# Hybrid decoder trunk: the norm scales of four norms spread through DRAM, the first SSD transposes tied behind products

## The chip, the cores and the metric

The kernel runs on one core of one Trainium2 chip. The metric is the device time of one execution in microseconds (us), taken as the median of several runs. The kernel before takes 2185.96, 2186.17 and 2187.34 us, median 2186.17. The profiled execution, which all rows of the profile come from, took 2185.88 us; its span from the first to the last instruction is 2184.1 us, with a mean granted TensorE clock of 0.999.

Engines are named as in the profile: PE is TensorE (PEld its weight loads), DVE is VectorE, ACT is ScalarE, POOL is GpSimd, SP is SyncE. An L with a number is a line of the kernel.

## The reference

The trunk has two residual layers for 256 tokens of width 2048, all in float32. Each layer is a mixer and a gated FFN, each behind an RMS norm; a last norm closes it.

```python
def rms_norm(x, w):
    xf = x.astype(jnp.float32)
    y = xf * lax.rsqrt(jnp.mean(xf * xf, axis=-1, keepdims=True) + EPS)
    return (y * w.astype(jnp.float32)).astype(x.dtype)
...
    for layer in range(DEPTH):
        hn = rms_norm(h, mix_norm_w[layer])
...
        h = h + mix.astype(h.dtype)
        f = conv_ffn(rms_norm(h, ffn_norm_w[layer]), ffn_w_gate[layer], ffn_w_up[layer],
                     ffn_conv_w[layer], ffn_conv_b[layer], ffn_w_down[layer])
        h = h + f.astype(h.dtype)
    return rms_norm(h, final_norm_w)
```

The even layer's mixer is stick-breaking attention beside a Mamba-2 SSD, the odd layer's a mixture of dilated attentions. The even mixer projects the input to q, k, v, a gate z, the SSD's inputs (through a causal convolution of width 4 and a SiLU) and 16 step sizes dt. The SSD part has a norm of its own (`ssm_norm_w`).

## The kernel before

Activations lie transposed: 16 tiles of 128 channels by 256 tokens. Every weight panel comes from DRAM in chunks of 128 x 1024 values (512 KB). `prep` (L135) loads one chunk by SP into one of 4 `raw` buffers, ACT casts it to a high half (L153), DVE subtracts to get the low half (L154), both into one of 3 `hl` buffers. `chan` (L218) then multiplies: 16 products per chunk, two accumulator banks, for each weight tile one product of the high half with both halves of x (512 columns) and one of the low half with the high half of x (256 columns), L225. 78% of the chain of work that ended last is L225.

The norm is not applied to x before the products. The weight of the norm goes into x; the factor per token (1 over the root of the mean square) is multiplied onto the results. `square` sums the squares; `stats` (L313) makes the scale: a product with a column of 1/D sums over the partitions (L321), then thirteen small DVE steps (L323, and L305 to L311 in `rsqrt`) give `rcol`, the scale with tokens on partitions, 128 x 2 values. The results have channels on partitions and need the scale along the free dimension, the same on all partitions: `rbc`, 128 x 256. `stats` makes it by two PE products of a broadcast column of `rcol` with the identity (L329, each two records in the trace) and an ACT copy out of PSUM (L333). `token_scale` (L336) runs `stats` in the background of the products, with `gap` ticks (one per chunk) between the two parts. It is used by the even mixer, both FFNs and the odd mixer. The SSD's inner norm calls `stats` itself (L1067). That makes five norms; the final norm is computed another way.

Uses of `rbc`: in the even mixer L904 and L922 (convolution inputs and gates, both DVE), in the FFN L671 (DVE) and L678 (POOL), in the odd mixer L839 and L845 (DVE).

The even mixer begins with `opening` (L165), 16 steps that compute the first values, dt, and four tiles of the convolution's inputs at once; its `token_scale` starts late, since the squares are summed during the opening. Right behind it stand, on DVE and ACT, the reading of the first values (L885, L887), the sums of the accumulators (L288 on ACT, L289 on DVE), the convolution (L904, ACT L907, three L909 per tile, ACT L911), the decays of the SSD (L948 to L968, then three products L974, L975, L977 and a trip of the row sums through DRAM, written by ACT at L984 and read back to all partitions by four POOL transfers of 512 KB at L989), and the casts and low halves of the next chunks.

`ssd` (L991) first transposes eight tiles, each in two halves of the tokens, in four groups of four (L1003, one PSUM bank per group), and DVE multiplies each group by dt (L1008).

The order on each engine is not the order of the source: a scheduler lays the instructions out, by priorities and its own estimates of time, wherever their inputs allow. `issue_after(i)` forbids it to place an instruction ahead of instruction `i`. So the first group of transposes, whose inputs are ready early, stands far ahead of the code around it. Engines run their list in order; semaphores make them wait for each other and for transfers.

Of the kernel before, what the change touches and what calls it, by code (L numbers as in the profile page):

```python
# [9 lines left out]
F32 = mybir.dt.float32  # L10
# [5 lines left out]
P = 128  # L16
T = 256
NT = T // P
# [50 lines left out]
class Trunk:  # L69
# [148 lines left out]
    def chan(self, accs, hl, xs, k0, start, stop):  # L218


        for nt in range(2):
            for k in range(CH):
                for w in range(2):
                    n = (2 - w) * T
                    self.nc.tensor.matmul(  # L225
                        accs[nt][:, :n], hl[w][:, k, nt * P : (nt + 1) * P], xs[k0 + k][:, :n],
                        start=start and k == w == 0, stop=stop and w == 1 and k == CH - 1,
                    )
# [81 lines left out]
            v.tensor_tensor(t, t, x, ALU.mult)  # L310
            v.scalar_tensor_tensor(y, t, 1.5, y, ALU.add, ALU.mult)  # L311

    def stats(self, sums, inv):  # L313


        nc = self.nc
        s = sums[0]
        self.then(nc.vector, "tensor_tensor", s[:, :T], s[:, :T], s[:, T:], ALU.add)
        ps = self.psum()
        for tt in range(NT):  # L320
            nc.tensor.matmul(ps[:, tt : tt + 1], s[:, tt * P : (tt + 1) * P], inv[:, 0:1], start=True, stop=True)  # L321
        ms = self.norm_tile("ms", NT)
        nc.vector.tensor_scalar(ms, ps[:, :NT], EPS, None, ALU.add)  # L323
        col = self.norm_tile("rcol", NT)
        self.rsqrt(col, ms, NT)
        yield col
        pb = self.psum()
        for tt in range(NT):
            nc.tensor.matmul(  # L329
                pb[:, tt * P : (tt + 1) * P], col[:, tt : tt + 1].broadcast_to([P, P]), self.ident, start=True, stop=True  # L330
            )
        bc = self.norm_tile("rbc")
        nc.scalar.copy(bc, pb[:, :T])  # L333
        yield bc

# [655 lines left out]
    def ssd(self, dt, o):  # L991


        nc = self.nc
        v = nc.vector
        conv = self.conv

        xdt = []
        for tt in range(NT):
            for g in range(2):  # L1000
                ps = self.psum()
                for i in range(4):
                    nc.tensor.transpose(  # L1003
                        ps[:, i * P : (i + 1) * P], conv[4 * g + i][:, tt * P : (tt + 1) * P], self.ident
                    )
                t = self.big("ssd", 14, F32)
                h0 = tt * SSH + 8 * g
                v.tensor_tensor(  # L1008
                    t.rearrange("p (h c) -> p h c", c=SSP), ps.rearrange("p (h c) -> p h c", c=SSP),
                    dt[:, h0 : h0 + 8].unsqueeze(2).broadcast_to([P, 8, SSP]), ALU.mult,  # L1010
                )
                xdt.append(t)
                yield
# [3 lines left out]
        for g in range(2):  # L1017
            b, cc = conv[8 + g], conv[10 + g]
            ps = self.psum()
            nc.tensor.matmul(ps[:, :T], b[:, :P], cc, start=True, stop=True)  # L1020
            nc.tensor.matmul(ps[:, T:W], b[:, P:], cc[:, P:], start=True, stop=True)
            t = self.t256("sc", 2, W)
# [6 lines left out]
        sums = []  # L1029
        ys = []  # L1030
        for j in range(SSH // 2):
            g = j // 4
# [4 lines left out]
            for i in range(2):  # L1037
                h = 2 * j + i
                for c in range(NT):
                    col = self.sums[:, c * SSH + h : c * SSH + h + 1]  # L1040
# [23 lines left out]
                self.square(sums, self.convs[j // 2])  # L1064
        yield
        yield
        st = self.stats(sums, self.invi)  # L1067
        next(st)
        yield
        yield  # L1070
        rbc = next(st)
        for j in range(8):
            t = self.t256("cv", 3)
# [173 lines left out]
```

## Time and profile before

| what | us |
|---|---|
| runs: lowest, median, highest | 2185.96, 2186.17, 2187.34 |
| profiled execution | 2185.88 |
| its span | 2184.1 |
| PE busy | 2174.2 |
| DVE busy | 1517.5 |
| ACT busy | 1167.1 |
| POOL busy | 96.8 |
| L225 products of x and panels: one record, mean | 0.333 |
| L329: 20 records, busy in all | 3.0 |
| L1003: 16 records, busy in all | 2.7 |

Matmuls are pipelined, so the duration of one record is longer than the distance between two starts; the chain of waits, which counts each stretch of time once, is better for prices. A line of the timeline holds the start, the duration, the engine, the line, the operation with its output and inputs, and in brackets the idle time before it with what ended it. A line of the chain holds start, time on the chain, engine, what is written and the line.

### The profile page before, as it was taken

To read this page: it belongs to the slowest core of one execution; us is meant where nothing else is said; L and a number is where in the kernel's file an instruction comes from. 1 tells how busy PE (TensorE), PEld (TensorE's weight loads), DVE (VectorE), ACT (ScalarE), POOL (GpSimd) and SP (SyncE) were. 2 spreads that over 40 slices of the span, in tenths; PEclk is the share of its full clock that TensorE was granted. 3 is DMA by queue.
4 is the path that set the end of the run, shared out by engine and by line. 5 is a ranking of instruction groups with operands and counts; after the bars stand their busy time and mean duration, and the time that the engine had idled before them with its cause. 6 is when DMAs were issued, how large, how long until landed. Compare 5 with 4: busy or idle time off the path is not lost.

```text
span 2184.1 us, 33866 instructions
## 1 busy us (share of the span) xinstructions
PE 2174.2 (100%) x13129; PEld 1934.0 (89%) x13129; DVE 1517.5 (69%) x2294; ACT 1167.1 (53%) x1709; POOL 96.8 (4%) x107
## 2 busy tenths in 40 slices
PE   9999999999999999999999999999999999999998
PEld 8888888888888888888888888888888888888998
DVE  8688766776767665555565556667676766687887
ACT  7566554655555554444454454546555555555554
POOL 0000000110101010000000000000010101000000
PEclk9999999999999999999999999999999999999999
DMA  7755566666666666666656555666666666666665
GB/s 252 242 173 151 168 187 192 191 193 194 194 195 193 195 194 194 193 193 194 193 175 181 175 172 177 184 193 189 185 193 193 194 193 194 194 202 199 206 205 162
DMA packets 117713, 417.54 MB, mean 191 GB/s; under 512 B 13072, under 2 KB 15408, under 8 KB 117552
## 3 DMA queue, kind: packets, MB, share of 16 engines
q1 hardware_dynamic: 116352, 412.48, 62.4%
q8 instruction: 102, 1.67, 0.3%
q0 software_dynamic: 576, 2.10, 0.3%
q10 hardware_dynamic: 624, 0.81, 0.1%
q14 instruction: 59, 0.48, 0.1%
HBM read 413.22 MB, written 2.11 MB: 190 GB/s over the span
## 4 chain that ended last, share of the span: by engine, by line
PE 98%; DVE 1%; ACT 0%; DMA 0%; issue 0%; SPq 0%; DVEq 0%
PE acc L225 78%; PE acc L518 5%; PE acc L424 4%; PE acc L526 3%; PE aux L542 2%; PE acc L542 1%; PE acc L235 1%; PE acc L198 1%; PE acc L242 1%; PE acc L190 0%; PE aux L779 0%; PE aux L810 0%; PE acc L200 0%; PE aux L801 0%; PE aux L1057 0%; DMA raw<-in_wfirst 0%
## 5 line engine op out<-in xcount | busy, mean ns | idle before, releaser
L225 PE MATMUL acc<-x,hl 128*128 128x512 f32 (+1 forms) x7680 | 1319.5, 333 | 0.3 <-DVE hl L154 0.3
L154 DVE TENSOR_TENSOR hl<-raw,hl 128x1024 fp32r<-128x1024 f32 x740 | 905.8, 1224 | 580.2 <-ACT hl L153 573.1
L225 PEld LDWEIGHTS acc<-x,hl 128*128 128x128 f32 x7680 | 1156.3, 188 | 151.1 <-issue 0.7
L153 ACT CAST hl<-raw 128x1024 fp32r<-128x1024 f32 x740 | 776.7, 1050 | 766.4 <-PE acc L225 530.4
L225 PE MATMUL acc<-act,hl 128*128 128x512 f32 (+1 forms) x1408 | 239.5, 332 | 0.0
L225 PEld LDWEIGHTS acc<-act,hl 128*128 128x128 f32 x1408 | 212.0, 188 | 27.4
L225 PE MATMUL acc<-o,hl 128*128 128x512 f32 (+1 forms) x1024 | 175.1, 333 | 0.0
L225 PEld LDWEIGHTS acc<-o,hl 128*128 128x128 f32 x1024 | 154.2, 188 | 20.0
L288 ACT COPY ev<-acc 128x256 f32<-128x256 f32 x244 | 90.8, 374 | 149.5 <-PE acc L225 148.5
L678 POOL TENSOR_TENSOR cv<-cv,rbc 128x256 f32<-128x256 f32 x88 | 93.6, 1082 | 1228.9 <-ACT cv L677 1228.9
L518 PE MATMUL acc<-hl,act 128*128 128x256 f32 x998 | 119.8, 278 | 0.0
L518 PEld LDWEIGHTS acc<-hl,act 128*128 128x128 f32 x998 | 117.4, 188 | 0.4
L289 DVE TENSOR_TENSOR ev<-acc,ev 128x256 f32<-128x256 f32 x244 | 102.2, 420 | 5.2 <-ACT ev L288 3.3
L424 PE MATMUL acc<-hl,x 128*128 128x512 f32 x384 | 90.5, 393 | 0.0
L424 PEld LDWEIGHTS acc<-hl,x 128*128 128x128 f32 x384 | 71.5, 188 | 14.8
L526 PE MATMUL acc<-hl,act 128*128 128x512 f32 x264 | 60.0, 389 | 0.0
L526 PEld LDWEIGHTS acc<-hl,act 128*128 128x128 f32 x264 | 49.5, 188 | 10.3
L688 DVE TENSOR_TENSOR ev<-ev,cv 128x256 f32<-128x256 f32 x88 | 38.3, 437 | 12.0 <-DVE ev L289 2.3
L677 ACT ACTIVATE cv<-cv,params 128x256 f32<-128x256 f32 x88 | 40.1, 503 | 0.1
L674 ACT ACTIVATE cv<-pad,params 128x256 f32<-128x256 f32 x88 | 39.9, 505 | 0.0
L671 DVE TENSOR_TENSOR pad<-ev,rbc 128x256 f32<-128x256 f32 x88 | 37.5, 426 | 3.0
L675 DVE SCALAR_TENSOR_TENSOR cv<-pad,params,cv 128x256 f32<-128x256 f32 x88 | 38.5, 479 | 0.0
(224 smaller groups left out, 1210.0 us busy)
## 6 DMA issues: line engine op xcount, KB each, us to landing
raw<-in_wg SPq DMA_DIRECT2D x176, 512.0 KB, 4.2
raw<-in_wu SPq DMA_DIRECT2D x176, 512.0 KB, 4.1
raw<-in_wd SPq DMA_DIRECT2D x176, 512.0 KB, 4.3
raw<-in_wev SPq DMA_DIRECT2D x76, 512.0 KB, 4.1
raw<-in_wod SPq DMA_DIRECT2D x64, 512.0 KB, 3.7
raw<-in_wevo SPq DMA_DIRECT2D x32, 512.0 KB, 4.2
raw<-in_wodv SPq DMA_DIRECT2D x32, 512.0 KB, 3.6
raw<-in_wodo SPq DMA_DIRECT2D x32, 512.0 KB, 3.6
```

The lines of the kernel that those rows point to most:

```text
L153: nc.scalar.copy(hi, raw)
L154: self.lo = nc.vector.tensor_tensor(lo, raw, hi.bitcast(F32), ALU.subtract)
L225: self.nc.tensor.matmul(accs[nt][:, :n], hl[w][:, k, nt * P : (nt + 1) * P], xs[k0 + k][:, :n], start=start and k == w == 0, stop=stop and ...
L288: nc.scalar.copy(t, acc[:, T:])
L289: nc.vector.tensor_tensor(t, acc[:, :T], t, ALU.add)
L424: self.nc.tensor.matmul(acc, part(xs[k0 + k], p), hl[:, k, w, :], start=start and n == k == 0, stop=stop and n == 2 and k == ch - 1,)
L518: mm(block(accs, tt, j), x, both(hl, w, k)[:, j], start=first, stop=stop and k == 1 and i == 2 and (two or j == 1),)
L526: mm(accs[tt][0].rearrange("p (j c) -> p j c", c=T), part(xs[2 * pair + k], p, tt), both(hl, w, k), start=start and i == k == 0, stop=stop ...
L542: mm(m[i] if i in m else block(accs, *own[i]), x[p], w[b][q], start=start and n == 0 and i not in own, stop=stop and n == 2 and i not in own)
L674: nc.scalar.activation(c, gp[:, 2:], AF.Copy, scale=w(2))
L677: self.last = nc.scalar.activation(c, c, AF.Silu, bias=self.par("fcb", l * FT + j))
L678: nc.gpsimd.tensor_tensor(c, c, self.rbc, ALU.mult)
```

## The change

Four norms (all with `token_scale`) no longer spread their scale by PE. Right after `rcol`, `stats` issues two transfers from POOL: one writes the 256 values to a DRAM tile, the other reads them back as one row for all 128 partitions, into `rbc`. The products L329 and the copy L333 remain only for the SSD's norm, which passes `soon=True`. The transposes of `ssd` are tied behind the last panel product that had been written when their code ran (`self.mm`).

```diff
@@ chan
-                    self.nc.tensor.matmul(
+                    self.mm = self.nc.tensor.matmul(
@@ stats
-    def stats(self, sums, inv):
+    def stats(self, sums, inv, soon=False):
...
         self.rsqrt(col, ms, NT)
+        bc = self.norm_tile("rbc")
+        if not soon:
+            back = self.dram.tile([NT, P], F32, name=self.nm("cols"))
+            nc.gpsimd.dma_start(back.rearrange("t p -> p t"), col)
+            nc.gpsimd.dma_start(bc, back.rearrange("t p -> (t p)").unsqueeze(0).broadcast_to([P, T]))
         yield col
+        if not soon:
+            yield bc
         pb = self.psum()
...
-        bc = self.norm_tile("rbc")
         nc.scalar.copy(bc, pb[:, :T])
@@ ssd
-                    nc.tensor.transpose(
-                        ps[:, i * P : (i + 1) * P], conv[4 * g + i][:, tt * P : (tt + 1) * P], self.ident
-                    )
+                    with self.tc.issue_after(self.mm.ins):
+                        nc.tensor.transpose(
+                            ps[:, i * P : (i + 1) * P], conv[4 * g + i][:, tt * P : (tt + 1) * P], self.ident
+                        )
@@ ssd, its norm
-        st = self.stats(sums, self.invi)
+        st = self.stats(sums, self.invi, soon=True)
```

Lines of the changed file are higher by 7 or 8 behind `stats`: L904 is L911 there, L909 is L916, L922 is L929, L951 and L952 are L958 and L959, L968 is L975, L974 is L981, L1003 is L1011; the two transfers are L330 and L331.

The change moves instructions. First DVE, just after the opening, before the change; `hl_666` is the weight buffer of chunk 2 of the products behind the opening (the count starts at 0), `rbc_548` the spread scale:

```order
L289 TENSOR_TENSOR ev_645<-acc_141,ev_645 128x256
L289 TENSOR_TENSOR ev_655<-acc_142,ev_655 128x256
L904 TENSOR_TENSOR pad_135<-ev_645,rbc_548 128x256
L904 TENSOR_TENSOR pad_136<-ev_655,rbc_548 128x256
L951 TENSOR_SCALAR s_601<-s_598 128x32
L154 TENSOR_TENSOR hl_666<-raw_665,hl_666 128x1024
L952 RECIPROCAL s_601<-s_601 128x32
```

And the same place after the change, where chunk 2's buffer is called `hl_665` and the scale `rbc_507`:

```order
L289 TENSOR_TENSOR ev_644<-acc_141,ev_644 128x256
L289 TENSOR_TENSOR ev_654<-acc_142,ev_654 128x256
L154 TENSOR_TENSOR hl_665<-raw_664,hl_665 128x1024
L958 TENSOR_SCALAR s_600<-s_597 128x32
L911 TENSOR_TENSOR pad_135<-ev_644,rbc_507 128x256
L959 RECIPROCAL s_600<-s_600 128x32
L911 TENSOR_TENSOR pad_136<-ev_654,rbc_507 128x256
```

The low half of chunk 2 now stands ahead of the two products with the scale. Some thirty rows further on DVE, before the change, with chunk 4's buffer `hl_742` and chunk 5's `hl_763`:

```order
L968 SCALAR_TENSOR_TENSOR s_620<-dt_134,s_618 128x16 x2
L909 SCALAR_TENSOR_TENSOR cv_691<-pad_135,params,cv_691 128x256
L909 SCALAR_TENSOR_TENSOR cv_701<-pad_136,params,cv_701 128x256
L289 TENSOR_TENSOR ev_729<-acc_575,ev_729 128x256
L909 SCALAR_TENSOR_TENSOR cv_701<-pad_136,params,cv_701 128x256
L922 TENSOR_TENSOR ev_729<-ev_729,rbc_548 128x256
L909 SCALAR_TENSOR_TENSOR cv_701<-pad_136,params,cv_701 128x256
L289 TENSOR_TENSOR ev_734<-acc_576,ev_734 128x256
L154 TENSOR_TENSOR hl_742<-raw_741,hl_742 128x1024
L922 TENSOR_TENSOR ev_734<-ev_734,rbc_548 128x256
L154 TENSOR_TENSOR hl_763<-raw_762,hl_763 128x1024
```

The same rows of DVE after the change, where these buffers are `hl_741` and `hl_762`:

```order
L975 SCALAR_TENSOR_TENSOR s_619<-dt_134,s_617 128x16 x2
L916 SCALAR_TENSOR_TENSOR cv_690<-pad_135,params,cv_690 128x256
L154 TENSOR_TENSOR hl_741<-raw_740,hl_741 128x1024
L916 SCALAR_TENSOR_TENSOR cv_690<-pad_135,params,cv_690 128x256
L916 SCALAR_TENSOR_TENSOR cv_700<-pad_136,params,cv_700 128x256
L289 TENSOR_TENSOR ev_728<-acc_574,ev_728 128x256
L916 SCALAR_TENSOR_TENSOR cv_700<-pad_136,params,cv_700 128x256
L929 TENSOR_TENSOR ev_728<-ev_728,rbc_507 128x256
L916 SCALAR_TENSOR_TENSOR cv_700<-pad_136,params,cv_700 128x256
L289 TENSOR_TENSOR ev_733<-acc_575,ev_733 128x256
L154 TENSOR_TENSOR hl_762<-raw_761,hl_762 128x1024
L929 TENSOR_TENSOR ev_733<-ev_733,rbc_507 128x256
```

Chunk 4's low half has moved up by seven operations of the convolution and the gates; chunk 5's has kept its place. Now PE, where chunk 4 begins, before the change (`acc_739` and `acc_740` are the two banks of the second job):

```order
L225 MATMUL acc_739<-x_151,hl_742 128x512
L225 MATMUL acc_740<-x_151,hl_742 128x512
L974 MATMUL aux_911<-s_620,consts 128x32
L975 MATMUL aux_911<-s_620,consts 128x16
L977 MATMUL aux_914<-consts,s_620 32x128
L1003 MATMUL aux_1378<-consts,ssd_644 128x128 x2
L1003 MATMUL aux_1378<-consts,ssd_686 128x128 x2
L225 MATMUL acc_739<-x_151,hl_742 128x256
```

After the change the three products of the decays stand one chunk later on PE (chunk 5, `hl_762`):

```order
L225 MATMUL acc_739<-x_207,hl_741 128x256
L225 MATMUL acc_738<-x_233,hl_762 128x512
L225 MATMUL acc_739<-x_233,hl_762 128x512
L981 MATMUL aux_910<-s_619,consts 128x32
L982 MATMUL aux_910<-s_619,consts 128x16
L984 MATMUL aux_913<-consts,s_619 32x128
L225 MATMUL acc_738<-x_233,hl_762 128x256
```

The first group of transposes has left that place. It now stands 382 panel products further on PE, at the end of a chunk and one chunk ahead of the second group:

```order
L225 MATMUL acc_1271<-x_465,hl_1336 128x512
L225 MATMUL acc_1271<-x_465,hl_1336 128x256
L1011 MATMUL aux_1377<-consts,ssd_643 128x128 x2
L1011 MATMUL aux_1377<-consts,ssd_685 128x128 x2
L225 MATMUL acc_1384<-x_151,hl_1387 128x512
L225 MATMUL acc_1384<-x_151,hl_1387 128x256
```

The other three groups stand where they stood. On ACT the four copies L333 are gone and some of the casts and copies near the opening change places; on POOL the two transfers of each norm stand ahead of that norm's first use.

## The prediction

> **What bounds the kernel now.** I read the page first: its span, its busy time by engine and the chain of work that ended last; then the groups of instructions for the product that the change removes.
>
> ```profile
> span 2184.1 us, 33866 instructions
> ...
> PE 2174.2 (100%) x13129; PEld 1934.0 (89%) x13129; DVE 1517.5 (69%) x2294; ACT 1167.1 (53%) x1709; POOL 96.8 (4%) x107
> ...
> PE 98%; DVE 1%; ACT 0%; DMA 0%; issue 0%; SPq 0%; DVEq 0%
> ...
> L329 PE MATMUL aux<-consts,rcol 128*128 128x128 f32 x20 | 3.0, 273 | 0.0
> ```
>
> TensorE (PE) carries 98% of the chain, so time is won only where PE has less to do or waits less. The removed product is 20 records, four for each of five norms. The change takes four norms' worth. Next, the chain of waits around such a product at the start of the first FFN:
>
> ```profile
> 373.91 4.08 PE acc L225 x24
> 377.99 0.44 PE aux L329 x4
> 378.44 13.62 PE acc L225 x80
> ```
>
> Here PE runs without a gap: a panel product takes 4.08/24 = 0.170 us, a chunk of 16 takes 2.72, and one norm's spreading product takes 0.44. Then the one stretch in which PE is not the bound, the start of the even mixer, in the same view:
>
> ```profile
> 37.69 0.47 ACT hl L153
> ...
> 38.64 0.36 ACT rbc L333
> 39.01 0.74 ACT v L885 x2
> 39.75 0.61 ACT ev L288 x3
> ...
> 40.69 0.94 ACT hl L153
> ...
> 41.88 0.33 DVE hl L154
> ...
> 43.01 0.35 DVE s L952
> ...
> 47.63 1.14 DVE hl L154
> ...
> 52.96 1.14 DVE hl L154
> ...
> 54.15 3.91 PE acc L225 x22
> ```
>
> From 37.69 to 54.15 the chain runs through ACT and VectorE (DVE). DVE has the convolution, the decays and the low halves of the weights (L154) to do in one order, and PE waits for the low half of chunk 4, which is written only at 52.96. I count chunks of the products from 40.20 on, from 0. The timeline of PE shows that wait:
>
> ```profile
> 51.73 0.30 PE L974 MATMUL aux<-s,consts 128*128 128x32 f32 x2
> 51.87 0.37 PE L975 MATMUL aux<-s,consts 128*128 128x16 f32 x2
> 52.17 0.41 PE L977 MATMUL aux<-consts,s 128*32 128x128 f32 x2
> 52.51 0.55 PE L1003 MATMUL aux<-consts,ssd 128*128 128x128 f32 x3
> 53.56 0.33 PE L1003 MATMUL aux<-consts,ssd 128*128 128x128 f32 x1 [0.50 <-ACT ssd L911]
> 54.15 0.38 PE L225 MATMUL acc<-x,hl 128*128 128x256 f32 x1 [0.26 <-DVE hl L154]
> ```
>
> The four early transposes (L1003) show a wait of 0.50 us for ACT, which is what the tie seems to remove. But behind them stands the later wait, for DVE: without the transposes PE would still resume at 54.15.
>
> **The products removed.** In the FFNs and the odd mixer they lie on the chain: 3 x 0.44 = 1.32 us gained, as long as the scales arrive in time. In the opening the fourth gains nothing at first. The timeline there, of DVE and of PE's weight loads:
>
> ```profile
> 39.91 0.37 DVE L887 SCALAR_TENSOR_TENSOR dt<-acc,rcol,params 128x16 f32<-128x16 f32 x2
> ...
> 40.20 4.79 PEld L225 LDWEIGHTS acc<-x,hl 128*128 128x128 f32 x28 [0.27 <-DVE dt L887]
> ```
>
> PE already waits at 40.20 for DVE's reading of the first values (L887). DVE is held by an L154 that follows the cast of 37.69, and that cast waits for a product that stands before L329. Ending the opening 0.44 earlier lengthens this wait. The copies L333 are hidden behind PE, except in the opening, where 0.36 us leave the ACT chain.
>
> **The order on DVE.** The order of the changed program (shown with the change) puts the third L154 ahead of the two products with the scale, and the L154 of chunk 4 ahead of seven operations of the convolution. The three products of the decays move behind chunk 4. So take one state: all of chunk 4, two products of chunk 5 and the three decay products are done. Before: 54.15 + 16 x 0.170 = 56.87. After: 82 products from 40.20, at the 0.175 us that the 66 before 51.73 took (11.53/66), plus 52.51 - 51.73 = 0.78, is 55.3. DVE must also have the low half of chunk 5 ready; before, it follows that of chunk 4:
>
> ```profile
> 54.33 2.37 DVE L154 TENSOR_TENSOR hl<-raw,hl 128x1024 fp32r<-128x1024 f32 x2
> ```
>
> The first of these two is chunk 5's, done at about 55.5. Its place in the list of DVE is nearly the same in both orders, so it comes at 55.5 again if DVE has not stood still meanwhile. The stretch gains 56.87 - 55.5 = 1.4 us, less the time d that DVE loses by waiting for the scale.
>
> **The tie.** The four moved transposes now stand where PE never waits. The chain gives their price from the second group:
>
> ```profile
> 121.98 0.44 PE aux L1003 x4
> ```
>
> So +0.44 us, certain. DVE reads their result only behind the second group's, whose place is unchanged, so nobody waits longer for them.
>
> **The trip through DRAM.** This decides d, and no row shows it: a POOL transfer of 256 values of 4 bytes, POOL's wait for it, and a POOL transfer of 128 KB. When must it be back? The last step of the scale on DVE and its first use, in the opening and in the first FFN:
>
> ```profile
> 36.31 0.16 DVE L311 SCALAR_TENSOR_TENSOR rcol<-nt,rcol 128x2 f32<-128x2 f32 x1
> ...
> 40.86 0.75 DVE L904 TENSOR_TENSOR pad<-ev,rbc 128x256 f32<-128x256 f32 x2
> ...
> 375.64 0.16 DVE L311 SCALAR_TENSOR_TENSOR rcol<-nt,rcol 128x2 f32<-128x2 f32 x1
> ...
> 383.89 0.43 DVE L671 TENSOR_TENSOR pad<-ev,rbc 128x256 f32<-128x256 f32 x1
> ```
>
> In the first FFN there are 8.1 us (383.89 - 375.80), and PE keeps a finished chunk in hand behind that; the odd mixer and the second FFN have the same pattern. On POOL the second transfer waits for the first; behind it stand only work of 55.38 (opening) and the FFN's products with the scale, which come after that use, so this wait delays nobody else. In the opening the scale is ready at 36.47. In the new order the use follows the third L154: the ACT pair L885 ends at 39.4 without L333, two of the L288 at 39.8, the cast at about 40.85, L154 and a small step at 42.2 or 42.3. So 5.8 us are free there, and each us beyond holds DVE, with every L154 queued behind it. The nearest rows for the price, from timeline, transfers and line views:
>
> ```profile
> 53.68 0.34 ACTq L984 DMA_DIRECT2D rows<-s  x1
> ...
> DMA to landing us min/median/max: 1.4/1.4/1.4
> ...
> 55.38 2.29 POOL L989 DMA_DIRECT2D sr<-rows  x4 [54.30 <-DMA rows<-s]
> ...
> L989 POOL DMA_DIRECT2D sr<-rows x4: 527/532/720, 55.4 to 57.1; - x4
> ...
> raw<-in_wev SPq DMA_DIRECT2D x7, 512.0 KB, 4.2
> ...
> sr<-rows POOLq DMA_DIRECT2D x4, 512.0 KB, 11.2
> ```
>
> A 16 KB write from ACT lands 1.4 us after its issue, and POOL follows 0.3 later. As quick a trip is 2 x (0.3 + 1.4) = 3.4 us. With a weight load's 4.2 for each it is 2 x (0.3 + 4.2) = 9.0. The 11.2 belongs to four broadcasts of 512 KB that crowd each other; I leave it as a far end. I take 2.8 per transfer, the middle of 1.4 and 4.2, since these are small but run beside the weights and are issued by POOL: 2 x (0.3 + 2.8) = 6.2 us. The scale is back at 36.47 + 6.2 = 42.7, so d = 0.4; at 3.4 us d = 0, at 9.0 us d = 3.2.
>
> The Trainium skill, "DMA: Bandwidth & Descriptors", section "Anatomy of one DMA — SWDGE (gpsimd) path", gives about 2.0 us fixed plus the bytes at 436 GB/s for a POOL transfer; by it the trip is an estimated 4.9 us with my waits, d is 0 and the sum 0.4 us better. No run here shows a POOL transfer of this size.
>
> **Sum.** -1.32 (three products) + 0.44 (transposes) - 1.4 + 0.4 (the stretch) = -1.9 us. The profiled execution took 2185.88 us, 1.78 more than its span; that makes 2184.0. The median of the runs is 0.29 higher, so 2184.3.
>
> **Rivals.** (1) *The trip is long and DVE becomes the wait.* For it: five L154 queue behind the waiting product, and a POOL transfer may be held while a DVE instruction runs. Priced by rows: 0.3 + 4.2 + one L154 of 1.22 is 5.7 per transfer, 11.4 for two; the scale is back at 47.9, d = 5.6, and the sum is -1.32 + 0.44 - 1.4 + 5.6 = +3.3, or 2189.5 with the 0.29 of the median. It decides from d = 2.3, a trip of 8.1 us: above that the kernel is slower than before. Against it: POOL's issues of 527 to 720 ns show no hold though they overlap the L154 of 54.33. The Trainium skill, "SBUF — State Buffer", section "A bandwidth-pool intuition that's wrong (but worth ruling out)", speaks against this change: a POOL-issued transfer of 620 ns took 3100 beside a DVE copy, since its descriptors wait for the port. By that rule the trip is an estimated 5 us longer than mine, d is 5.4, and the time is this rival's; the 527 to 720 ns do not bear it out. Chance 0.17.
>
> (2) *The gain of the stretch is given back to the weights' transfers.* The four 512 KB broadcasts of the decays start about 2.8 us later (their products end at 55.3, not 52.5), while PE is 1.0 us ahead. The rows that show how thin the cover is:
>
> ```profile
> 63.74 1.05 ACT L153 CAST hl<-raw 128x1024 fp32r<-128x1024 f32 x1 [3.23 <-DMA raw<-in_wev]
> ...
> 71.05 1.22 DVE L154 TENSOR_TENSOR hl<-raw,hl 128x1024 fp32r<-128x1024 f32 x1
> ```
>
> ACT waits 3.23 us for weights there, and the low half of chunk 11 is ready at 72.3, when PE reaches it at 54.15 + 14 x 0.170 + 6 x 2.72 = 72.85: 0.6 us to spare. If nothing there moves forward, the whole 1.0 is lost: 2185.3. Against it: the L154 of chunk 4 is earlier by some 3 us, so its refill is too. Chance 0.2.
>
> (3) *The change does not bring the order's gain*, because the low half of chunk 3 (47.63 before), now two steps further back, holds PE instead: then -1.32 + 0.44 = -0.9 remains, again 2185.3. Chance 0.05.
>
> **Numbers.** My forecast has 0.58: 2184.3. Its own ends are d = 0 (2183.9) and d = 3.2 (2187.1). The range reaches down to 2183.0 for the spread of the runs (2185.96 to 2187.34) and up to 2188.0, which leaves out most of rival 1. A measurement of this kernel tells about 0.2%, 4.4 us, from no change. No case gains that much, since even d = 0 is under 3 us: 0.02 for faster. Slower by more needs d of 6.7 or more, the far end of rival 1, or scales that are late in the FFNs too: 0.05. The rest, 0.93, is the same.
>
> **What would show it.** Right: the spreading product shows only the SSD norm's four records; DVE's first product with the scale waits under 1 us for a transfer; PE's gap near 51.7 is gone and the decay products stand near 54.5; the transposes appear in one group more near 118; the FFN starts show no wait of DVE for the scale. Wrong: DVE idle for 2 us or more at that product, a new PE wait for L154 between 45 and 56 or between 63 and 75, or waits for the scale at the FFNs.

## The result, and the profile after

The changed kernel takes 2213.36 us (median of 4 runs, 2212.74 to 2213.94), beside 2186.07 (4 runs, 2185.78 to 2187.34) for the kernel before: a ratio of 1.0126, 95% interval 1.0114 to 1.0138. It is slower by 27 us. The forecast was 2184.3, in a range from 2183.0 to 2188.0; the measured time lies far above that range. The page of the changed kernel shows where to look:

```profile
span 2212.2 us, 33850 instructions
...
PE 2181.4 (99%) x13113; PEld 1939.0 (88%) x13113; DVE 1517.3 (69%) x2294; ACT 1164.9 (53%) x1705; POOL 103.0 (5%) x115
...
PE 95%; DMA 3%; DVE 1%; issue 1%; ACT 0%; DVEq 0%; POOL 0%; POOLq 0%
```

DVE and ACT do as much as before, and POOL 6 us more. What is new is DMA with 3% of the chain, where it had 0%; the lines of the chain give 2% to `cols<-rcol`, the write, and 1% to `rbc<-cols`, the read. The two transfers by their lines, L330 the write of 256 values, L331 the read to all partitions; the last line of each group is the time from the issue to the landing:

```profile
L330 POOL DMA_DIRECT2D cols<-rcol x4: 718/745/886, 37.1 to 1494.6; - x4
...
DMA to landing us min/median/max: 8.6/9.0/9.5
```

```profile
L331 POOL DMA_DIRECT2D rbc<-cols x4: 554/556/560, 46.7 to 1503.5; - x4
...
  DVE pad L678: 15.3, 2
  DVE pad L911: 9.3, 1
  DVE q L846: 7.6, 1
...
DMA to landing us min/median/max: 5.1/5.5/5.8
```

The 1 KB write takes 9.0 us, the 128 KB read 5.5. All four first uses of the scale wait for the read, in the FFNs and the odd mixer too. The timeline of the opening (start, length, instruction, idle time before it and what ended it):

```profile
36.62 0.16 DVE L311 SCALAR_TENSOR_TENSOR rcol<-nt,rcol 128x2 f32<-128x2 f32 x1
...
37.09 0.89 POOL L330 DMA_DIRECT2D cols<-rcol  x1 [36.01 <-DVE rcol L311]
...
46.70 0.56 POOL L331 DMA_DIRECT2D rbc<-cols  x1 [8.73 <-DMA cols<-rcol]
51.91 0.42 DVE L911 TENSOR_TENSOR pad<-ev,rbc 128x256 f32<-128x256 f32 x1 [9.29 <-DMA rbc<-cols]
52.37 0.51 ACT L914 ACTIVATE cv<-pad,params 128x256 f32<-128x256 f32 x1 [10.58 <-DVE pad L911]
...
54.53 1.22 PE L225 MATMUL acc<-x,hl 128*128 128x512 f32 x2 [5.35 <-ACT hl L153]
...
58.62 7.12 PE L225 MATMUL acc<-x,hl 128*128 128x256 f32 x32 [2.87 <-DVE hl L154]
```

The scale is ready at 36.78 and used at 51.91: a trip of 15.1 us. DVE stands still for 9.29 of them. ACT stands still too, for 10.58, since its convolution step waits for that product; and the high half of the next weights (L153) is queued behind the step on ACT as the low half is on DVE. So PE waits first for ACT's half (5.35), then for DVE's (2.87). In the first FFN, the same view:

```profile
385.59 0.16 DVE L311 SCALAR_TENSOR_TENSOR rcol<-nt,rcol 128x2 f32<-128x2 f32 x1
386.04 0.73 POOL L330 DMA_DIRECT2D cols<-rcol  x1 [8.06 <-DVE rcol L311]
...
395.79 0.56 POOL L331 DMA_DIRECT2D rbc<-cols  x1 [9.01 <-DMA cols<-rcol]
401.38 0.43 DVE L678 TENSOR_TENSOR pad<-ev,rbc 128x256 f32<-128x256 f32 x1 [8.04 <-DMA rbc<-cols]
401.72 0.42 DVE L289 TENSOR_TENSOR ev<-acc,ev 128x256 f32<-128x256 f32 x1
...
402.19 2.08 PE L225 MATMUL acc<-x,hl 128*128 128x512 f32 x5 [4.73 <-DVE ev L289]
```

The product with the scale (L678) waits 8.04 us. Behind it on DVE stands the L289 that empties a second accumulator bank, and PE needs that bank: it stops for 4.73 us. PE stopped at 397.46, so a scale 4.7 us earlier, a trip of some 10.9 us instead of 15.6, would have cost PE nothing here. The waits of PE over the whole run:

```profile
PE acc L225 <- DVE ev L289: 13.0, 3, 4.7
PE acc L225 <- ACT hl L153: 5.3, 1, 5.3
PE acc L225 <- DVE hl L154: 2.9, 1, 2.9
```

That is 21 us, less 1.3 for the products that went; it does not make 28. The rest lies in work that took longer: by the two pages PE was busy for 7.2 us more (2181.4 after 2174.2), though sixteen records went. The reason is the granted clock (PEclk), which the table by windows of 4 us shows around the wait of the first FFN. Its columns are the window, its length, PE's busy time with its records, the granted clock, the DMA share and GB/s; first the changed kernel, then the one before:

```profile
394.00:398.00 4.00, 3.46 (x21) 1.00 0.59 156
398.00:402.00 4.00, 0.00 (x0) 0.69 0.67 219
402.00:406.00 4.00, 3.81 (x12) 0.50 0.31 63
406.00:410.00 4.00, 4.00 (x24) 0.96 0.59 189
```

```profile
402.00:406.00 4.00, 4.00 (x25) 1.00 0.70 231
406.00:410.00 4.00, 4.00 (x25) 1.00 0.63 176
```

After the wait PE runs at 0.50 until about 406: the 12 records from 402.19 on take 3.8 us where 12 x 0.170 = 2.0 is normal. The wait of 4.73 us costs 4.73 + 1.8 = 6.5. The Trainium skill, "TensorE: Matmul & The Clock Gate", section "Part 1: The HAM clock gate (the "warmup" mystery)", says that TensorE drops to half its clock after an idle window of about 3.4 us and needs about 3.4 us of work to come back; the rows above agree with it roughly. Behind the other two late scales PE waited 4.30 and 3.95 us and then ran at 0.50 for longer, 6.1 and 5.7 us; behind the two waits of the opening the clock is 0.50 too, until about 61.6.

The last small step of `rcol` (L311) marks each norm in the timeline of DVE, so the loss can be laid out by stage:

| from one norm's scale to the next | before | after | difference |
|---|---|---|---|
| start to mixer (36.31; 36.62) | 36.3 | 36.6 | +0.3 |
| mixer to SSD norm (222.82; 232.78) | 186.5 | 196.2 | +9.7 |
| SSD norm to first FFN (375.64; 385.59) | 152.8 | 152.8 | 0.0 |
| first FFN to odd mixer (1094.66; 1111.10) | 719.0 | 725.5 | +6.5 |
| odd mixer to second FFN (1470.72; 1494.15) | 376.1 | 383.1 | +7.0 |
| second FFN to the end (2184.1; 2212.2) | 713.4 | 718.1 | +4.7 |

27.9 of the 28.1 us lie in the four stages that begin with a trip. The last row is the least certain: in kernels below that leave the scale of the second FFN to PE, this stage lasts from 712.6 to 714.7 us.

### The profile page after: what moved, and what is told of

Its sections match the earlier page's. It is cut to its first block, busy times and chain, and to the rows that moved or that the text cites. A ratio compares the mean times of both kernels' runs of the same rounds, so it can differ in the third digit from the quotient of the medians.

```text
span 2212.2 us, 33850 instructions
## 1 busy us (share of the span) xinstructions
PE 2181.4 (99%) x13113; PEld 1939.0 (88%) x13113; DVE 1517.3 (69%) x2294; ACT 1164.9 (53%) x1705; POOL 103.0 (5%) x115
## 4 chain that ended last, share of the span: by engine, by line
PE 95%; DMA 3%; DVE 1%; issue 1%; ACT 0%; DVEq 0%; POOL 0%; POOLq 0%
PE acc L225 75%; PE acc L525 5%; PE acc L431 4%; PE acc L533 3%; DMA cols<-rcol 2%; PE aux L549 1%; PE acc L549 1%; PE acc L235 1%; DMA rbc<-cols 1%; PE acc L198 1%; PE acc L242 1%; PE acc L190 0%; PE aux L786 0%; PE aux L817 0%; PE acc L200 0%
## 5 line engine op out<-in xcount | busy, mean ns | idle before, releaser
L225 PE MATMUL acc<-x,hl 128*128 128x512 f32 (+1 forms) x7680 | 1328.8, 335 | 21.6 <-DVE ev L289 13.0
L225 PEld LDWEIGHTS acc<-x,hl 128*128 128x128 f32 x7680 | 1163.3, 189 | 175.3 <-DVE ev L289 13.9
L154 DVE TENSOR_TENSOR hl<-raw,hl 128x1024 fp32r<-128x1024 f32 x740 | 906.2, 1225 | 578.8 <-ACT hl L153 571.5
L153 ACT CAST hl<-raw 128x1024 fp32r<-128x1024 f32 x740 | 776.8, 1050 | 762.8 <-PE acc L225 529.5
L225 PE MATMUL acc<-act,hl 128*128 128x512 f32 (+1 forms) x1408 | 239.5, 333 | 0.0
L225 PEld LDWEIGHTS acc<-act,hl 128*128 128x128 f32 x1408 | 211.7, 188 | 27.6
L225 PE MATMUL acc<-o,hl 128*128 128x512 f32 (+1 forms) x1024 | 175.1, 333 | 0.0
L225 PEld LDWEIGHTS acc<-o,hl 128*128 128x128 f32 x1024 | 154.4, 188 | 19.9
L289 DVE TENSOR_TENSOR ev<-acc,ev 128x256 f32<-128x256 f32 x244 | 102.2, 420 | 5.5 <-ACT ev L288 3.7
L431 PEld LDWEIGHTS acc<-hl,x 128*128 128x128 f32 x384 | 71.5, 188 | 14.8
L678 DVE TENSOR_TENSOR pad<-ev,rbc 128x256 f32<-128x256 f32 x88 | 37.5, 426 | 18.2 <-DMA rbc<-cols 15.3
```

The source lines that it names most:

```text
L153: nc.scalar.copy(hi, raw)
L154: self.lo = nc.vector.tensor_tensor(lo, raw, hi.bitcast(F32), ALU.subtract)
L225: self.mm = self.nc.tensor.matmul(accs[nt][:, :n], hl[w][:, k, nt * P : (nt + 1) * P], xs[k0 + k][:, :n], start=start and k == w == 0, sto ...
L289: nc.vector.tensor_tensor(t, acc[:, :T], t, ALU.add)
L431: self.nc.tensor.matmul(acc, part(xs[k0 + k], p), hl[:, k, w, :], start=start and n == k == 0, stop=stop and n == 2 and k == ch - 1,)
```

## The experiments

Theory S, formed from the profile: the trip is long because `rcol` is written as 256 pieces of 4 bytes. Rivals: POOL is slow to issue (P); the transfers stand in a queue behind the weights, whatever they hold (Q); the order and the tie are to blame, not the trip (O). Each batch has its own runs of the kernel before, named with it.

### Which transfer is slow

Eight unused transfers were added to the kernel before, in the first FFN, each tied behind a product so that they run one at a time.

```diff
+        with self.tc.issue_after(self.pl.ins):
+            nc.gpsimd.dma_start(four.rearrange("t p -> p t"), col)
...
+            nc.gpsimd.dma_start(d([P, NT]), col)
...
+            nc.scalar.dma_start(d([NT, P]).rearrange("t p -> p t"), col)
...
+            nc.gpsimd.dma_start(d([NT, P]), self.ident[:NT, :])
+            nc.gpsimd.dma_start(d([P, P]), self.ident)
+            nc.gpsimd.dma_start(self.pbc, four.rearrange("t p -> (t p)").unsqueeze(0).broadcast_to([P, T]))
```

> The kernel before (scales spread by PE), with eight transfers added in the first FFN that nobody waits for; each time to landing is read from the trace. Theory S (small pieces): a DMA engine takes its pieces of 4 bytes one after another, 9.0 us / 16 = 0.56 us each. Then 256 pieces of 4 bytes from POOL land after about 9 us, the same from ACT after about 9 too, 128 pieces of 8 bytes after 4.5 to 5.5 from either engine, two pieces of 512 bytes after 1 to 3, and 128 pieces of 512 bytes show whether a piece's number (4.5) or its smallness (under 3) counts. Theory P (POOL issues slowly): the three writes from POOL all take 7 to 9 us, those from ACT 1.4 to 3. Theory Q (waiting behind the weights): all eight lie between 4 and 9 us, without regard to shape or engine. The broadcast read of 128 KB: 5.5 us from POOL; under P 2 to 3 from ACT, under S and Q again about 5.

From issue to landing, by line:

| transfer | issued by POOL | issued by ACT |
|---|---|---|
| write, 256 pieces of 4 bytes | 9.6 | 10.4 |
| write, 128 pieces of 8 bytes | 4.6 | 5.0 |
| write, 2 pieces of 512 bytes | 3.3 | |
| write, 128 pieces of 512 bytes (64 KB) | 4.4 | |
| broadcast read, 128 KB | 4.3 | 4.0 |

The same 1 KB takes 9.6 us in pieces of 4 bytes and 3.3 in two pieces (1 to 3 was expected). The broadcast read takes less than the 5.5 expected. P falls (ACT is no faster), and Q falls (64 KB on the same queue lands in 4.4).

### The tie alone

```diff
-                    nc.tensor.transpose(
-                        ps[:, i * P : (i + 1) * P], conv[4 * g + i][:, tt * P : (tt + 1) * P], self.ident
-                    )
+                    with self.tc.issue_after(self.mm.ins):
+                        nc.tensor.transpose(
+                            ps[:, i * P : (i + 1) * P], conv[4 * g + i][:, tt * P : (tt + 1) * P], self.ident
+                        )
```

> The tie of the transposes alone, all scales spread by PE as before. The order on DVE is that of the kernel before, so by the prediction's own argument PE still waits for chunk 4's low half near 54 us and the four transposes cost 0.44 us at their new place: +0.4 us, within 0.1% of before. Rival: the wait of 0.50 us for ACT was a real loss and goes: -0.5 us. If the tie were part of the loss, it would show several us here.

It takes 2186.01 us beside 2185.27, a ratio of 1.0006 (0.9997 to 1.0015): no difference that can be measured. PE does wait for DVE at the same place as before, as the prediction said:

```profile
51.92 0.41 PE L984 MATMUL aux<-consts,s 128*32 128x128 f32 x2
53.91 6.45 PE L225 MATMUL acc<-x,hl 128*128 128x256 f32 x27 [1.58 <-DVE hl L154]
```

But the profiled execution shows a price that the prediction did not have. Its windows of 2 us, and those of the kernel before:

```profile
52.00:54.00 2.00, 0.41 (x3) 1.00 0.00 0
54.00:56.00 2.00, 2.00 (x10) 0.77 0.54 129
56.00:58.00 2.00, 2.00 (x8) 0.50 0.89 305
58.00:60.00 2.00, 2.00 (x13) 0.88 0.91 233
```

```profile
52.00:54.00 2.00, 1.38 (x9) 1.00 0.00 0
54.00:56.00 2.00, 1.85 (x11) 1.00 0.42 90
56.00:58.00 2.00, 2.00 (x14) 1.00 0.86 305
58.00:60.00 2.00, 2.00 (x14) 1.00 0.74 211
```

In the kernel before, the four transposes fell into PE's wait and broke it up, and the clock stayed at 1.00. With the transposes gone, 1.6 us without work were followed by a stretch at half clock. These are single executions, and the stretch does not seem to come each time: of the 11 runs with the tie, three have a mean granted clock of 0.998 and eight have 0.999. From the mixer's norm to the SSD norm this profile takes 188.6 us, 2.1 more than before. Over all the runs of the kernel the difference is 0.7 us and cannot be told from none.

### The trip alone, and the trip with the write issued by ACT

The first has the change without the tie. The second has all of the change, with one word altered:

```diff
-            nc.gpsimd.dma_start(back.rearrange("t p -> p t"), col)
+            nc.scalar.dma_start(back.rearrange("t p -> p t"), col)
```

> The trip through DRAM alone, transposes untied as before. If the trip is the whole loss: +26 to +28 us (2212 to 2214). If the tie has a part in it, for instance by the order on DVE: clearly less, under +22.

> The change with the write of the 256 values issued from ACT instead of POOL; the read stays on POOL. Theory S: the write still lands after about 9 us, loss within 3 us of the change's 27. Theory P: it lands after 1.4 to 3 us, the trip is 9 instead of 15 us, the FFN and odd waits (13 us) go and the opening's fall by some 6: about +7 us. Theory Q: as S.

The trip alone takes 2215.58 us, a ratio of 1.0138 (1.0123 to 1.0154); with the write issued by ACT 2215.47, 1.0137 (1.0124 to 1.0151). Both lose some 30 us, 2 to 3 more than was expected, but the intervals overlap that of the change. So the trip is the whole loss and O falls. ACT's write lands in 9.6 us at the median, POOL's in 9.0: the issuing engine does not matter in the kernel either.

### What makes the pieces slow

```diff
+            nc.gpsimd.dma_start(d([NT, P]).rearrange("t p -> p t"), col)
...
+            nc.gpsimd.dma_start(d([NT, P, P])[:, :, 0].rearrange("t p -> p t"), col)
...
+            nc.gpsimd.dma_start(d([P, 1]), col[:, :1])
+            nc.gpsimd.dma_start(d([NT, P, P]).rearrange("t p c -> p t c"), self.dbias[:, :T].rearrange("p (t c) -> p t c", c=P))
```

> The kernel before with six unused POOL writes to DRAM in the first FFN, one at a time: 256 pieces of 4 bytes (twice, first and last), 256 pieces of 4 bytes that lie 512 bytes apart in DRAM, 128 pieces of 4 bytes, 256 pieces of 512 bytes (128 KB), 128 pieces of 1 KB (128 KB). Known so far: 256 x 4 bytes land in 9.6 us, 128 x 8 bytes in 4.6, 128 x 512 bytes in 4.4. Theory S1 (the number of pieces that each transfer is cut into sets the time, whatever they hold): 256 x 4 bytes 9 to 10 us in both placements, 128 x 4 bytes about 4.6, 256 x 512 bytes about 9, 128 x 1 KB about 4.5. Theory S2 (pieces that are smaller than some size are slow because neighbours share a line of the memory): spaced out, 256 x 4 bytes fall to 5 us or less, and 256 x 512 bytes takes about 5. Theory S3 (small pieces are slow by themselves): 256 x 4 bytes 9 to 10 in both placements, 256 x 512 bytes about 5, as 128 x 1 KB.

The line of the side-by-side pieces and that of the same pieces 512 bytes apart:

```profile
L343 POOL DMA_DIRECT2D pr<-rcol x1: 778/778/778, 426.3 to 426.3; - x1
...
DMA to landing us min/median/max: 11.3/11.3/11.3
```

```profile
L347 POOL DMA_DIRECT2D pr<-rcol x1: 757/757/757, 469.8 to 469.8; - x1
...
DMA to landing us min/median/max: 4.1/4.1/4.1
```

256 pieces of 4 bytes take 11.3 and 9.7 us side by side, but 4.1 when they lie 512 bytes apart; 128 pieces of 4 bytes side by side 8.7; 256 pieces of 512 bytes 4.2 and 128 of 1 KB 4.1. Neither the number of pieces (S1) nor their smallness (S3) makes the time: neighbourhood in DRAM does (S2). How near is too near was asked next:

```diff
+        for w in (1, 2, 4, 8, 16, 1, 0):
...
+                    nc.gpsimd.dma_start(d([NT, P, w])[:, :, 0].rearrange("t p -> p t"), col)
```

> The kernel before with seven unused POOL writes of the 128 x 2 column in the first FFN, one at a time, in this order: 256 pieces of 4 bytes that lie 4, 8, 16, 32 and 64 bytes apart in DRAM, then 4 bytes apart again, then 128 pieces of 8 bytes side by side. Known: 4 bytes apart 9.6 to 11.3 us, 512 bytes apart 4.1, the 8-byte pieces 4.6. Theory S4 (two pieces that share one 8-byte word wait for each other): 8 bytes apart and more land in 4 to 5 us. Theory S5 (pieces that share one line of 64 bytes wait for each other, 8-byte pieces being merged): 4 to 32 bytes apart 8 us or more, only 64 apart about 4. Theory S6 (a slow fall with spacing): times between, each step shorter.

| distance of the 4-byte pieces | 4 B | 8 B | 16 B | 32 B | 64 B | 4 B again | 128 pieces of 8 B, side by side |
|---|---|---|---|---|---|---|---|
| us to landing | 10.7 | 6.9 | 4.9 | 2.7 | 3.7 | 11.1 | 5.0 |

The time falls with each doubling up to 32 bytes and not beyond, and pieces of 8 bytes side by side are nearer to 4-byte pieces 16 bytes apart than to those 8 apart. S4 and S5 fall; the fall with distance (S6) fits. It looks as if pieces that share 32 bytes of DRAM wait for each other: 8, 4, 2 and 1 of them there give 10.7, 6.9, 4.9 and 2.7. The number of pieces counts as well: with as many sharing 32 bytes, 128 pieces take 8.7 where 256 take 9.7 to 11.3, and 128 of 8 bytes take 5.0 where 256 of 4 bytes take 6.9. That is a reading of two profiles, with a single transfer at most distances. The Trainium skill, "DMA: Bandwidth & Descriptors", section "Specifications", says that a DMA below 512 bytes does a read-modify-write. A queue of such writes at one place would give this fall, but no run here shows the queue; by size alone the rule does not give it, since 4-byte pieces 32 bytes apart land in 2.7.

### The change without small pieces

One PE transpose turns the column into two rows, and ACT copies them to SBUF; POOL then writes two pieces of 512 bytes. The read and the tie are the change's.

```diff
+            nc.tensor.transpose(pt[:NT, :P], col, self.ident)
+            nc.scalar.copy(row, pt[:NT, :P])
-            nc.gpsimd.dma_start(back.rearrange("t p -> p t"), col)
+            nc.gpsimd.dma_start(back, row)
```

> The change with the four-byte pieces taken away: one PE transpose turns the 128 x 2 column of the scale into 2 x 128, ACT copies it to SBUF, and POOL writes it as two pieces of 512 bytes; the broadcast read is the changed kernel's. Theory S (the four-byte pieces are the cost): the write lands in 3 to 4 us instead of 9, the trip with transpose and copy takes 9 to 11 us instead of 15; in the FFNs and the odd mixer that is in time (PE's wait for L289 under 1 us in sum, 13.0 in the changed kernel), in the opening DVE waits about 4 to 5 us for the scale (9.3 in the changed kernel); the whole is 0 to 5 us over the kernel before, about 2188 on a chip where that takes 2185.3. Rival T (any trip through DRAM, or the broadcast read, disturbs the weights): still over 2200.

It takes 2186.92 us beside 2185.33, a ratio of 1.0006 (0.9997 to 1.0016). The 27 us are gone. The write lands in 3.3 us at the median, the read in 4.2 (5.5 in the changed kernel), and PE's waits are:

```profile
PE acc L225 <- DVE hl L154: 2.8, 1, 2.8
PE aux L163 <- DVE z L160: 1.1, 1, 1.1
PE acc L225 <- DVE dt L898: 0.4, 1, 0.4
```

L289 is gone from the list. In the opening DVE still waits:

```profile
41.22 0.58 POOL L335 DMA_DIRECT2D rbc<-cols  x1 [3.08 <-DMA cols<-row]
...
45.78 0.42 DVE L915 TENSOR_TENSOR pad<-ev,rbc 128x256 f32<-128x256 f32 x1 [3.13 <-DMA rbc<-cols]
```

The scale is ready at 36.48 and used at 45.78, a trip of 9.3 us, of which DVE waits 3.13. Theory S holds in all its numbers but that one, which is a little smaller than expected; rival T falls.

### The trip in the FFNs and the odd mixer only

```diff
-        st = self.stats(sums, self.invd)
+        st = self.stats(sums, self.invd, soon=wait > 2)
```

> The change with the opening's scale spread by PE as before; the trip stays in both FFNs and the odd mixer, the tie stays. Theory A (each PE wait for L289 costs what the trace shows, 4.7, 4.3 and 4.0 us, and the opening costs the other half of the loss): 13.0 - 1.3 (three products) + 0.4 (tie) = 12 us over the kernel before, 2197 on a chip where that takes 2185.3, so the opening alone costs about 16. Rival B (the opening's waits are taken in by later slack, and the three late scales are nearly all of the loss): 2208 or more. Rival C (FFN waits are hidden by weight prefetch that catches up): 2190 or less.

2208.10 us beside 2185.33: +22.8, a ratio of 1.0100 (1.0083 to 1.0117). Theory A, 12 us, is refuted, and so is C. The three waits are there as A had them (14.6 us in sum), but A priced them at their length. The half clock behind each (0.50 after all three waits) is what A left out. By the norm marks of this run the stages from the three late scales are longer than before by 6.8, 7.3 and 7.0 us, 21 in sum. B's number, 2208 or more, was met, but its reason is not what the stages show: in the changed kernel the opening does cost, 9.7 us in its own stage against 0.5 here. The three late stages cost 18.2 us there and 21.2 here, and most of that difference is in the last stage (4.7 and 7.0); why is open.

### Can a better version be had?

Two ideas of the case were tried on the kernel before. One gives the opening the DVE order that the change gave it, by doing the second pair of convolutions two chunks later; with it went the tie and a spread by transposes of half the records:

```diff
-        self.products(jobs, xs, before=[lambda: convdone(0)(accs[1]), lambda: convdone(1)(accs[2])])
+        self.products(jobs, xs, before=[lambda: convdone(0)(accs[1]), lambda: None, lambda: None, lambda: convdone(1)(accs[2])])
...
-            nc.tensor.matmul(
-                pb[:, tt * P : (tt + 1) * P], col[:, tt : tt + 1].broadcast_to([P, P]), self.ident, start=True, stop=True
-            )
+            nc.tensor.transpose(pb[:, tt * P : (tt + 1) * P], col[:, tt : tt + 1].broadcast_to([P, P]), self.ident)
```

> The kernel before with the tie, each norm's spreading done by two transposes instead of two full-precision products (two records instead of four), and the second pair of convolutions of the even mixer put two chunks later in the products' list, so that DVE writes the low halves of chunks 3 to 5 ahead of its operations. Theory G (the opening of the mixer is bound by DVE's order, as the prediction had it): PE's wait of 2 us and more near 51 to 54 us goes, -1.0 to -2.0 us, and five norms x 0.22 us of records fall away, about -1: 2182.3 to 2183.7 on a chip where the kernel before takes 2185.3. Rival H (PE then waits for weights or for the convolution instead): 2184.5 to 2187.

2207.86 us beside 2185.33, a ratio of 1.0102 (1.0087 to 1.0117): both theories wrong. PE has no new wait; its panel products are slower, 288 records per 50 us in the first FFN where the kernel before has 296. So the two edits were run apart, the transposes alone first, then the later convolution with the tie.

> The kernel before with one edit: each norm's scale is spread by two PE transposes (two records) instead of two full-precision products (four records). Theory T1 (the slow pace of the first FFN in the late kernel comes from the transposes): 2205 or so on a chip where the kernel before takes 2185.3, with 288 panel records per 50 us in the first FFN where before has 296. Theory T2 (it comes from the later convolution or from the tie): five norms x 0.22 us = 1.1 us faster at most, 2184 to 2185.5, and 296 records per 50 us.

> The late kernel without the transposes as spreading: the kernel before with the tie, and the second pair of convolutions of the even mixer two chunks later in the products' list. Theory T1 (the transposes make the first FFN's pace): PE's wait of some 2 us near 51 to 54 is gone and the pace is 296 records per 50 us, so 2183.5 to 2185 on a chip where the kernel before takes 2185.3. Theory T2 (the later convolution makes it): 288 records per 50 us and about 2206.

The transposes alone take 2209.34 beside 2186.85 (1.0103, 1.0089 to 1.0116), the later convolution with the tie 2186.50 (0.9998, 0.9989 to 1.0008). The slow pace of the first FFN comes with the transposes. In the windows of that kernel (products of L225 alone; the transposes of the first FFN's norm run at 380.71):

```profile
360.00:370.00 10.00, 10.00 (x60) 1.00 0.64 196
...
400.00:500.00 100.00, 100.00 (x573) 1.00 0.63 190
...
1000.00:1100.00 100.00, 100.00 (x573) 1.00 0.61 188
...
1700.00:1800.00 100.00, 100.00 (x590) 1.00 0.65 194
```

From the transposes on, the products run at 573 per 100 us instead of some 590, for more than 700 us, at a granted clock of 1.00 and without a wait. Only the first FFN is that slow, though all five norms have the new transposes: by the norm marks its stage takes 739.7 us (719.0 before), but the one behind the opening 186.5 (186.5), the one behind the odd mixer's norm 376.0 (376.1) and the one behind the second FFN's 713.6 (713.4). The one behind the SSD norm is 1.6 us longer, 1.3 of it two waits of PE for L154. So the transposes alone are not enough for it. Why, stays open; the single 2-row transpose of the version above does not do it (295 records in the window of 380 to 430).

The later convolution takes PE's wait near 52 us away altogether, and gains nothing that can be measured. From the mixer's norm to the SSD norm it takes 186.6 us, before it was 186.5. The trace shows where the gain goes. The first line below holds the panel products of this kernel from the decay products to the first transposes, the second those of the kernel before from 55.74 us to its second group of transposes:

```profile
70.78 47.87 PE L225 MATMUL acc<-x,hl 128*128 128x512 f32 x272
```

```profile
55.74 66.24 PE L225 MATMUL acc<-x,hl 128*128 128x256 f32 x389
```

One product takes 47.87/272 = 0.176 us here and 66.24/389 = 0.170 before, so the 272 products lose 1.5 us, at a granted clock of 1.00 and without a wait of PE. That is the slow pace of the first FFN again, with no transposed spreading in this kernel; its cause is open here too.

The other idea keeps the part that should pay: two pieces of 512 bytes in the FFNs and the odd mixer, the opening by PE, no tie.

> The part of the change that should pay, in the form that the chip liked: in both FFNs and the odd mixer the scale is turned by one PE transpose, copied by ACT, written as two pieces of 512 bytes and read back as a broadcast; the opening's scale is spread by PE as before; no tie. The prediction's term (0.44 us of PE for each spreading product on the path, less one transpose record of some 0.1) gives 3 x 0.3 = 0.9 us faster than the kernel before, 2184.4 where that takes 2185.3, which the timing can hardly tell from no change. Rival: a broadcast read of 128 KB disturbs the weights and PE waits for L289: 2188 or more.

2185.67 us beside 2186.85, a ratio of 0.9996 (0.9987 to 1.0004): no difference that can be measured. PE has no wait for L289. By the norm marks the first FFN and the odd mixer each take 0.16 to 0.17 us less than before, which is the 0.44 of the removed product less the 0.27 that the transpose in its place takes on the chain (some 0.1 was expected for it, so 0.3 us of gain). So no version was found that beats the kernel before.

## Why the prediction was wrong

**The bound and the products removed.** Right as far as the runs show: in the last version the two stages that can be compared are 0.16 and 0.17 us shorter, which is 0.44 - 0.27 with the transpose in its place counted. The condition, "as long as the scales arrive in time", is what failed.

**The trip.** This is the step that failed, and its working shows how: 2.8 us per transfer as "the middle of 1.4 and 4.2", so 6.2 for the trip. In the four norms it was 14.8 to 15.6. The read's 5.5 us, 4.3 in the probe, is above the upper end of 4.2 but near it. The write's 9.0 is twice that end. Both neighbouring rows were chosen by bytes (16 KB in 1.4 us, 512 KB in 4.2), and the 1 KB write was put between them. But both move long runs (the 16 KB are 32 rows of 512 bytes); this write moves 256 single values that lie side by side in DRAM. No row of the profile before showed such a transfer, and the upper end for the whole trip, 9.0 us, was a guess that looked like a bound. The fixed 2.0 us of the Trainium skill, "DMA: Bandwidth & Descriptors", section "Anatomy of one DMA — SWDGE (gpsimd) path", which made 4.9 for the trip, falls further short; the 3.3 us for two pieces is nearer to it. Even with the right trip the prediction's sum would have been too small: d = 9.29 in it gives -1.32 + 0.44 - 1.4 + 9.29 = +7.0 us. The other 20 us are the two steps that follow and the half clock.

**ACT behind the scale, and the FFNs that hide the trip.** The sum let only DVE wait; in the opening ACT waited as well, and PE for both. That the FFNs have time enough was wrong by the same number as the trip. The 8.1 us to the first use and PE's spare bank give a break-even near 10.9 us, which a trip of 9 us meets (rows of the 512-byte version: no wait for L289) and one of 15.6 does not.

**Rival 1** named the mechanism rightly, DVE waiting for the scale with the weights' halves queued behind. Its price did not come near: d was 9.29 us instead of 5.6, ACT's queue was not counted, and the three later norms stood only in the chance of a larger loss, 0.05. The cause it offered, a POOL transfer held by DVE's port, is not it: ACT's write is as slow, and in the probes POOL's transfers of 512 bytes a piece and more land in 3.3 to 4.4 us. So the rule cited there from the Trainium skill, "SBUF — State Buffer", section "A bandwidth-pool intuition that's wrong (but worth ruling out)", is not what acts here.

**What a wait of PE costs.** No step had this. Each wait was priced at its length, but PE comes back at half clock: 1.8 us on top of 4.73 in the first FFN.

**The tie.** Its +0.44 us and the later wait behind the transposes came true. That nothing else hung on them did not: by the two profiles they had kept PE's clock up through that wait.

**The gain of the stretch, -1.4.** Not reached in the change, since DVE stood still. In the version with the later convolution PE's wait is gone and no gain shows: the products behind it run at 0.176 us instead of 0.170 and give 1.5 us back. So even with d = 0 this term would probably not have been reached, for a reason that none of the rivals names.

**Rivals 2 and 3** cannot be judged, since the trip covered their place.

## What to carry to other kernels

Price a transfer by its pieces and where they lie, not by its bytes: a column of single values written side by side to DRAM is the slow case, and a transpose in front of it is the cheap cure. Count for every new wait what is queued behind the waiter on each engine, ACT as well as DVE, and add the stretch at half clock that PE pays after a wait of some us. When a change hangs on one price that no row shows, its range must be worked out to where the sign turns in each stage, and the upper end must not be taken for a bound.

## What the runs showed of the hardware

- The slow write holds up others. For the window from its issue to near its landing in the first FFN, the changed kernel's DMA shows this, the weights' queue q1 being busy for 92.5% and moving little:

```profile
DMA packets 222, 0.73 MB, mean 76 GB/s; under 512 B 48, under 2 KB 48, under 8 KB 221
...
q1 hardware_dynamic: 189, 0.71, 92.5%
...
raw<-in_wg SPq DMA_DIRECT2D x2, 512.0 KB, 10.0
```

  The kernel before moves 163 GB/s between the same times, with landings of 3.6 to 4.3 us. The spacing probes agree: weight loads landed after 10.2 and 10.0 us (median) beside the pieces 4 bytes apart (the weights `in_wu`), 5.1 and 4.9 beside those 8 bytes apart, and 3.4 to 4.8 beside those 16 bytes apart and more.
- A gap of 1.6 us in PE's work was followed, about 1.2 us after work resumed, by some 3.4 us at half clock (0.77, 0.50 and 0.88 in three windows of 2 us of the profile with the tie alone). In the version with two pieces of 512 bytes a wait of 2.83 us was followed by windows of 0.51 and 0.64. The Trainium skill, "TensorE: Matmul & The Clock Gate", in the section cited above, names an idle window of about 3.4 us; here less was enough.
- Panel products have a slower pace, 3% below the usual one, at the same granted clock of 1.00 and without waits. Two full-width transposes of a broadcast column in place of two products brought it on for the whole first FFN, but not behind the other norms; the later convolution brought it on for 48 us of the even mixer. So saving two records can cost far more than the records, and an edit on PE must be timed as a whole.
